# A two-layer attention trunk on one core: the mask of a tenth group on VectorE, other buffer counts, another order of issue

## The chip, the core and the metric

The kernel runs on one core of one Trainium2 chip. A core has TensorE (PE) for matmuls, VectorE (DVE), ScalarE (ACT) and GpSimd (POOL) for elementwise work, and SyncE (SP), which here issues all the transfers between memory and the core's on-chip buffers. Each engine runs its own list of instructions in order and waits for others at semaphores. The metric is the time of one execution on the device, in microseconds (us); lower is better.

## The reference

The input x is 256 tokens by 1024 in float32. Two layers run one after the other, and then a final RMSNorm:

```
h = x
for i in 0, 1:
    hn = rmsnorm(h, norm_g[i])
    q, k, v, z = split(hn @ w_in[i])           # 16 heads of 64
    q, k = rope(q), rope(k)
    o = attention_i(q, k, v)                   # see below
    h = h + (o * silu(z)) @ w_out[i]
out = rmsnorm(h, final_g)
```

Layer 0 has 2 key heads, a sliding window of 128 keys, and one learned logit per head (a sink) that takes part in the softmax. Layer 1 has 4 key heads and attends in blocks of 256 keys; with 256 tokens there is only the token's own block, so it is plain causal attention. All weights are float32.

## The kernel before

**Weights.** The weights stream through the core once, in chunks of 128x1024 (512 KB). `load` (L90) takes a raw buffer `wraw` (one of NRAW) and lets SP issue the transfer. `split` turns a chunk into two of a reduced matmul format: ScalarE copies it to `whi` (L114), and VectorE subtracts that from the raw chunk to give `wlo` (L115); there are NHI and NLO buffers of these. Each copy waits for the subtraction of the chunk before it (PACE). Seven chunks (NATIVE) are not split and go to TensorE as they are (L149).

**Projections.** The activations stand transposed in SBUF, as 8 tiles of 128 features by 256 tokens, each split in the same way into a high and a low part (`quad`, L170 and L171). A 128x128 block of weights then takes three matmuls: high by high (L151), high by low (L152), low by high (L153). The same three stand at L290 to L292 for v of layer 1, at L450 to L452 for the output projection of layer 0, and at L487 to L489 for that of layer 1, which is computed in rows.

**Norms.** The norm's factor is taken out of the projections. The squares of the 8 tiles (`square`) are made by GpSimd (L176) for the tiles in SQP and by ScalarE (L178) otherwise, and added up by GpSimd (L181) in NACC accumulators. `stats` sums them over features by matmuls against a column of ones (L190), takes the power -1/2 on GpSimd and spreads the result over the features (L197).

**Attention.** `attn` handles 12 groups (layer, c, b, u): a half c of the heads, a block b of 128 queries, and for b = 1 a quarter u of the heads. A group has four heads with 256 keys, or (b = 0) eight heads with 128 keys. Its steps are:

- scores (`sc`, L351), matmuls with 64 rows of contraction;
- mask and maximum: for the groups in TTM, one VectorE operation a head, which adds the mask, writes the result and keeps the extreme (L355); otherwise two matmuls that add the mask in place (L361) and one VectorE reduction (L363);
- exponentials on ScalarE (L373 for TTM groups, L375 otherwise), reciprocal of the sums (L378), scaling on ScalarE for groups in PSC (L381), on VectorE otherwise (L383);
- transposes on TensorE (`tr`, L389), copied out by VectorE for groups in PEV (L392), by ScalarE otherwise (L394);
- P V products (`o`, L404), matmuls that write 64 columns of the array;
- the gate: times silu(z) (L410), and the split of the result into high (ScalarE, L416) and low (GpSimd for GLP, VectorE otherwise, L417).

silu(z) is made from a tanh (L432 to L438; the last steps on GpSimd for the parts in SZP), the rotary products by VectorE or, for RPL, GpSimd.

**What sets the order.** No order is written out by hand. A scheduler issues each engine's instructions by a priority, and every stage has one: layer times 100 plus an entry of PRI0 or PRI1 (`sq0` the split of q's weights of half 0, `a1` the attention of half 1, `o0` the output projection of half 0, and so on). ORDERS gives the order of the three groups of a half. So the tables of numbers at L24 to L42 decide what stands behind what on each engine.

Of the kernel before, what the change touches and what calls it, by code (L numbers as in the profile page):

```python
# [20 lines left out]
SYNC = mybir.DependencyInfo(mybir.DependencyClass.Sync, mybir.DependencyReason.DATA)  # L21
PACE = 1
NATIVE = (1, 2, 5, 6, 10, 13, 31)
RPL = [(0, 'k'), (0, 0, 0), (1, 'k'), (1, 0, 0), (1, 1, 0)]  # L24
GLP = [(0, 0, 0, 1), (0, 0, 1, 0), (0, 1, 0, 0), (0, 1, 0, 1), (1, 0, 1, 0), (1, 1, 0, 1)]
SZP = [(0, 0, 0), (0, 0, 1), (0, 0, 2), (0, 1, 2), (0, 1, 3), (1, 0, 0), (1, 0, 1), (1, 0, 2), (1, 0, 3), (1, 1, 1), (1, 1, 2)]
PSC = [(0, 0, 0, 0), (0, 0, 0, 1), (0, 0, 1, 0), (0, 0, 1, 1), (0, 1, 1, 1), (1, 0, 1, 0), (1, 0, 1, 1), (1, 1, 0, 0), (1, 1, 1, 0), (1, 1, 1, 1)]
PEV = [(0, 0, 0, 1), (0, 0, 1, 0), (0, 1, 0, 0), (0, 1, 0, 1), (1, 0, 0, 1), (1, 0, 1, 0), (1, 0, 1, 1), (1, 1, 0, 0), (1, 1, 0, 1), (1, 1, 1, 0), (1, 1, 1, 1)]
NRAW, NHI, NLO = 10, 6, 5
PRI0 = {'xf': -37.2, 'hi': -428.1, 'sr': -212.6, 'tr': -201.4, 'skv': -239.2, 'st': -202.2, 'kv': -40.0, 'sq0': 117.0, 'q0': 61.8, 'sz0': -423.6, 'z0': 22.4, 'a0': -231.3, 'sq1': 114.4, 'q1': -33.8, 'a1': -409.0, 'sz1': -356.7, 'z1': 57.5, 'so0': -315.8, 'o0': 144.9, 'so1': 106.2, 'o1': -413.8, 'r0': -105.6, 'r1': 19.7, 'rk': -221.8, 'p0': 21.4, 'p1': -32.3, 'e0': -419.0, 'e1': -270.7, 'f0': -176.2, 'f1': -172.3}  # L30
PRI1 = {'xf': -32.2, 'r0': 100.5, 'r1': 41.1, 'tr': 65.9, 'skv': 75.5, 'st': 15.9, 'kv': -179.8, 'sq0': -132.0, 'q0': 96.7, 'sz0': -35.0, 'z0': 217.1, 'a0': 44.0, 'sq1': -436.9, 'q1': 120.3, 'a1': -261.3, 'sz1': -243.0, 'z1': 33.9, 'so0': 29.9, 'o0': 69.6, 'so1': -254.9, 'o1': 34.0, 'rk': -306.8, 'p0': 14.1, 'p1': -192.3, 'e0': 71.7, 'e1': -119.0, 'f0': -280.2, 'f1': -10.4}
NPT = 6
NMM, NTR, NSC = 3, 2, 1
NW = 9
ORDERS = [[[(1, 0), (0, 0), (1, 1)], [(1, 0), (0, 0), (1, 1)]], [[(0, 0), (1, 1), (1, 0)], [(0, 0), (1, 1), (1, 0)]]]
STEP = 0.1
TTM = [(0, 0, 1, 0), (0, 0, 1, 1), (0, 1, 0, 0), (0, 1, 1, 0), (0, 1, 1, 1), (1, 0, 0, 0), (1, 0, 1, 1), (1, 1, 0, 0), (1, 1, 1, 1)]
SQP = [(0, 0), (0, 1), (0, 3), (0, 5), (1, 1), (1, 5), (1, 6)]
NACC = [2, 2]
PVZ = 0  # L40
EPS = 1e-05
NEG = -1e+30  # L42
# [3 lines left out]
def trunk(ctx: ExitStack, tc: tile.TileContext, xT, gf, sinks, consts, masks, wkva, w, out):  # L46
# [7 lines left out]
    @contextmanager  # L54
    def at(p):
        old = tc.cur_priority
        tc.cur_priority = int(p * 1000)
        yield
        tc.cur_priority = old
# [98 lines left out]
    def split_h(layer, k, hs):  # L158
        whole = any(26 * layer <= j < 26 * layer + 20 for j in NATIVE)
        if k == 0:  # L160
            xf.append(act.tile([P, KT, S], F32, name="xf", bufs=1) if whole else None)
        if k % 2 == 0:
            q = quads()
            hs += [q[:, 0], q[:, 1]]
        hi, lo = hs[k][:, 0], hs[k][:, 1]
        gc = g[:, layer, k:k + 1]
        if whole:
            with at(100 * layer + (PRI0, PRI1)[layer]["xf"] + 0.5 * k):
                nc.scalar.activation(xf[layer][:, k], h[:, k], AF.Copy, scale=gc)  # L169
        nc.scalar.activation(hi, h[:, k], AF.Copy, scale=gc)  # L170
        nc.vector.scalar_tensor_tensor(lo, h[:, k], gc, hi.bitcast(F32), op0=OP.mult, op1=OP.subtract)  # L171

    def square(layer, k):
        q = work.tile([P, S], F32, name="sq", bufs=4)
        if (layer, k) in SQP:
            nc.gpsimd.tensor_mul(q, h[:, k], h[:, k])  # L176
        else:
            nc.scalar.activation(q, h[:, k], AF.Square)  # L178
        if k >= NACC[layer]:
            a = acc[layer][k % NACC[layer]]  # L180
            nc.gpsimd.tensor_add(a, a, q)  # L181
        else:
            acc.setdefault(layer, []).append(q)
# [18 lines left out]
    for k in range(KT):  # L202
        with at(PRI0["hi"] + 0.5 * k):
            split_h(0, k, hs)
        with at(PRI0["sr"] + 0.5 * k):
            square(0, k)

    for layer in range(2):
# [8 lines left out]
        B = 100 * layer  # L217
        PRI = (PRI0, PRI1)[layer]

# [12 lines left out]
        def rope(aps, pool=False, out=None):  # L232
            n = sum(x.shape[1] for x in aps)
            t1 = work.tile([P, n, S], F32, name="t1") if out is None else out
            t2 = work.tile([P, n, S], F32, name="t2")
            n = 0
            for x in aps:
                m = x.shape[1]
                nc.vector.stream_shuffle(t2[:, n:n + m], x, [(i + 16) % 32 for i in range(32)])
                nc.vector.tensor_mul(t1[:, n:n + m], x, csr[:, 0, None].to_broadcast([P, m, S]))  # L240
                n += m
            eng = nc.gpsimd if pool else nc.vector
            eng.tensor_mul(t2, t2, csr[:, 1, None].to_broadcast([P, n, S]))
            eng.tensor_add(t1, t1, t2)
            return t1
# [54 lines left out]
        def q_part(c, pq):  # L300
            qs = act.tile([P, 4, S], F32, name="qs", bufs=2)
            for u in range(2):
                rope(pq[u], (layer, c, u) in RPL, qs[:, 2 * u:2 * u + 2])
            return qs
# [7 lines left out]
        tc.cur_priority = int(1000 * (B + PRI["rk"]))  # L312
        kr = rope([pk[:, :nkv // 2]], (layer, "k") in RPL)
        for i in range(2):
# [16 lines left out]
        def attn(c, b, u, qs):  # L331
# [14 lines left out]
            sc = psum.tile([P, 2, 512], F32, name="sc", bufs=NSC).rearrange("p r (i k) -> p r i k", i=np_)  # L346
            wide = (layer, c, b, u) in TTM
            for n in range(nh):
# [30 lines left out]
            for n in range(nh):  # L379
                if (layer, c, b, u) in PSC:  # L380
                    nc.scalar.activation(p[:, n], p[:, n], AF.Copy, scale=ri[:, n:n + 1])  # L381
# [3 lines left out]
            for j in range(2):  # L385
# [4 lines left out]
                pT = work.tile([P, 4, P], F32, name="pT", bufs=NPT)  # L390
                if (layer, c, b, u) in PEV:
                    ie = nc.vector.tensor_copy(pT, pt)  # L392
# [18 lines left out]
            for v in us:  # L411
# [4 lines left out]
                last[0] = nc.scalar.activation(gh, gv, AF.Copy)  # L416
                (nc.gpsimd if (layer, c, v, b) in GLP else nc.vector).tensor_sub(gl, gv, gh.bitcast(F32))  # L417

        def zproj(c):
            with at(B + PRI["sz%d" % c]):  # L420
                hw = split(jz[c])
            with at(B + PRI["z%d" % c]):
                for f in range(4):
# [5 lines left out]
                    with at(B + PRI["e%d" % c]):  # L429
# [3 lines left out]
                        nc.scalar.activation(th, z, AF.Tanh)  # L433
                        if (layer, c, f) in SZP:
                            nc.gpsimd.tensor_mul(th, th, z)  # L435
# [76 lines left out]
        def attn_c(c, qs):  # L512
            for i, (b, u) in enumerate(ORDERS[layer][c]):
                with at(B + PRI["a%d" % c] + STEP * i):
                    attn(c, b, u, qs)
# [84 lines left out]
```

## Time and profile before

| | us |
|---|---|
| median of 3 runs (219.52 to 219.86) | 219.74 |
| the profiled execution | 219.47 |
| its span, first to last instruction on the core | 217.7 |
| TensorE busy | 210.3 |
| VectorE busy | 156.0 |
| ScalarE busy | 137.8 |
| GpSimd busy | 59.5 |

The profiled execution is one run under the hardware profiler; its time exceeds the span by what lies before the first and after the last recorded instruction. Busy is the time in which an engine works on an instruction. An engine whose busy time is nearly the span can still be waiting in one place; what it waits for is told by the view of waits, and what a single piece adds to the end by the chain of waits, which goes back from the last instruction to whatever released it.

### The profile page before, as it was taken

Reading aid. Unit: us, or ns where it says so; the run is one execution under the profiler, and the core shown is the slowest. Engines: PE = TensorE matmul, PEld = TensorE weight load, DVE = VectorE, ACT = ScalarE, POOL = GpSimd, SP = SyncE. Lnnn points to the kernel's source line nnn. Section 1 sums busy time; section 2 is a strip of 40 time slices with the busy share of each in tenths; the row PEclk is TensorE's granted clock in tenths of the full one; section 3 lists DMA queues with packets and bytes.
Section 4 is the critical chain, followed back from the end, with each engine's and each line's share of the span. In section 5 each row is a group of like instructions: output and inputs, shape, how many; then the busy total and the mean of one; then the engine's idle time right before and its main releaser. Section 6 shows DMA issues by size and latency. Waiting matters only on the chain.

```text
span 217.7 us, 4176 instructions
## 1 busy us (share of the span) xinstructions
PE 210.3 (97%) x1533; PEld 185.4 (85%) x1533; DVE 156.0 (72%) x359; ACT 137.8 (63%) x335; POOL 59.5 (27%) x67
## 2 busy tenths in 40 slices
PE   8999999999999999999999999999999999999990
PEld 3879999896798989899999999999799997777780
DVE  3437978987488995768864577799655998585462
ACT  6683179698879576429931554567888997352221
POOL 2561440014401046003920182130440047000331
PEclk9999999999999999999999999999999999999998
DMA  6999999365041336345552664643530000000022
GB/s 173 278 386 411 408 400 321 133 199 184 5 148 47 96 98 193 105 131 161 190 144 89 211 232 114 222 120 133 172 118 3 0 3 0 0 0 3 0 96 96
DMA packets 10244, 31.71 MB, mean 146 GB/s; under 512 B 1264, under 2 KB 2160, under 8 KB 10224
## 3 DMA queue, kind: packets, MB, share of 16 engines
q1 hardware_dynamic: 10224, 31.45, 43.3%
q8 instruction: 12, 0.20, 0.3%
q14 instruction: 8, 0.07, 0.1%
HBM read 30.39 MB, written 1.05 MB: 144 GB/s over the span
## 4 chain that ended last, share of the span: by engine, by line
PE 89%; DMA 2%; SPq 2%; DVE 2%; issue 1%; ACT 1%; POOL 1%; POOLq 0%
PE mm L151 13%; PE mm L153 12%; PE mm L152 12%; PE mm L149 9%; PE sc L351 6%; PE o L404 6%; PE tr L389 5%; PE mm L451 4%; PE mm L452 4%; PE mm L450 4%; PE mm L487 3%; PE mm L489 3%; PE mm L488 2%; DMA hg<-xT 2%; SPq L96 1%
## 5 line engine op out<-in xcount | busy, mean ns | idle before, releaser
L115 DVE TENSOR_TENSOR wlo<-wraw,whi 128x1024 fp32r<-128x1024 f32 (+2 forms) x49 | 62.2, 1272 | 17.2 <-ACT whi L114 13.8
L114 ACT ACTIVATE whi<-wraw 128x1024 fp32r<-128x1024 f32 (+2 forms) x49 | 49.6, 1021 | 38.8 <-DVE wlo L115 18.3
L151 PE MATMUL mm<-quad,whi 128*128 128x256 f32 x224 | 66.4, 298 | 0.4 <-ACT whi L114 0.4
L152 PE MATMUL mm<-quad,whi 128*128 128x256 f32 x224 | 64.4, 288 | 0.0
L153 PE MATMUL mm<-quad,wlo 128*128 128x256 f32 x224 | 64.0, 288 | 0.0
L151 PEld LDWEIGHTS mm<-quad,whi 128*128 128x128 f32 x224 | 42.8, 191 | 2.3 <-issue 1.1
L153 PEld LDWEIGHTS mm<-quad,wlo 128*128 128x128 f32 x224 | 42.6, 191 | 1.2 <-issue 1.1
L152 PEld LDWEIGHTS mm<-quad,whi 128*128 128x128 f32 x224 | 42.8, 191 | 0.7
L435 POOL TENSOR_TENSOR th<-th,z 128x256 f32<-128x256 f32 x11 | 10.3, 936 | 56.2 <-ACT th L433 56.2
L373 ACT ACTIVATE p<-p,nm 128x256 f32<-128x256 f32 (+1 forms) x48 | 21.3, 444 | 5.0 <-DVE nm L355 4.9
L149 PE MATMUL mm<-xf,wraw 128*128 128x256 f32 x96 | 23.3, 380 | 0.3 <-ACT xf L169 0.3
L149 PEld LDWEIGHTS mm<-xf,wraw 128*128 128x128 f32 x96 | 17.3, 190 | 2.5 <-ACT xf L169 0.6
L452 PE MATMUL mm<-quad,wlo 128*128 128x256 f32 x64 | 18.4, 287 | 0.0
L451 PE MATMUL mm<-quad,whi 128*128 128x256 f32 x64 | 18.3, 286 | 0.0
L450 PE MATMUL mm<-quad,whi 128*128 128x256 f32 x64 | 18.3, 286 | 0.0
L381 ACT ACTIVATE p<-p,ri 128x256 f32<-128x256 f32 (+1 forms) x44 | 16.8, 458 | 1.4 <-DVE ri L378 1.3
L389 PE MATMUL tr<-cst,p 128*128 128x128 f32 x96 | 15.4, 273 | 0.0
L351 PE MATMUL sc<-ks,qs 64*128 64x256 f32 (+1 forms) x128 | 15.2, 348 | 0.0
L171 DVE SCALAR_TENSOR_TENSOR quad<-hg,quad 128x256 fp32r<-128x256 f32 x16 | 9.3, 601 | 6.5 <-ACT quad L170 6.5
L487 PE MATMUL mm<-whi,quad 128*128 128x512 f32 (+2 forms) x36 | 13.9, 385 | 0.0
L404 PE MATMUL o<-pT,vs 128*64 128x256 f32 x96 | 13.7, 395 | 0.0
L488 PE MATMUL mm<-wlo,quad 128*128 128x512 f32 (+2 forms) x36 | 13.3, 373 | 0.0
(110 smaller groups left out, 378.0 us busy)
## 6 DMA issues: line engine op xcount, KB each, us to landing
wraw<-w SPq DMA_DIRECT2D x50, 512.0 KB, 4.7
wraw<-wkva SPq DMA_DIRECT2D x2, 512.0 KB, 8.4
out<-of SPq DMA_DIRECT2D x4, 256.0 KB, 2.2
wraw<-w SPq DMA_DIRECT2D x3, 256.0 KB, 3.9
hg<-xT SPq DMA_DIRECT2D x2, 256.0 KB, 6.0
wraw<-gf SPq DMA_DIRECT2D x1, 512.0 KB, 3.6
hg<-xT SPq DMA_DIRECT2D x3, 128.0 KB, 3.4
cst<-consts SPq DMA_DIRECT2D x1, 320.0 KB, 8.5
```

Source lines behind the costliest of these rows:

```text
L114: ia = nc.scalar.activation(a[:, c0:c1], r[:, c0:c1], AF.Copy)
L115: ib = nc.vector.tensor_sub(b[:, c0:c1], r[:, c0:c1], a[:, c0:c1].bitcast(F32))
L149: nc.tensor.matmul(ps, wh, x, start=start, stop=stop)
L151: nc.tensor.matmul(ps, wh, xh, start=start, stop=False)
L152: nc.tensor.matmul(ps, wh, xl, start=False, stop=False)
L153: nc.tensor.matmul(ps, wl, xh, start=False, stop=stop)
L351: nc.tensor.matmul(sc[:, par, i], qs[half, 2 * us[0] + i, b * P:(b + 1) * P], ks[half, (h0 + n) // per, :nk], start=i == 0, stop=wide and ...
L389: nc.tensor.transpose(pt[:, n], p[:, n0 + n, kt * P:(kt + 1) * P], ident)
L404: im = nc.tensor.matmul(po[64 * par:64 * par + 64, i0:i0 + 2], vs[:, kt, (h0 + 2 * i0) // per], pTs[j][:, par::2], start=st, stop=sp)
L450: nc.tensor.matmul(ps, wh, gh, start=k == 0, stop=False)
L451: nc.tensor.matmul(ps, wh, gl, start=False, stop=False)
L452: nc.tensor.matmul(ps, wl, gh, start=False, stop=k == 3)
```

## The change

The change touches only tables of numbers, at the same lines as before. The mask of group (1, 1, 1, 0), the last of the kernel, moves from TensorE to VectorE (TTM, nine groups to ten). The raw weight buffers go from 10 to 7, the high ones from 6 to 8. Two squares of layer 0 go from GpSimd to ScalarE (SQP). The squares of layer 1 are added up in one accumulator, not two (NACC). Scaling on ScalarE (PSC) takes in the groups (0,1,0,0) and (0,1,1,0). The evictions in PEV, the gate's low parts in GLP, the rotary products in RPL and the last steps of silu in SZP are dealt out differently between VectorE, ScalarE and GpSimd. In layer 1 the first half takes its groups in another order (ORDERS). Nearly every priority is different.

```diff
-RPL = [(0, 'k'), (0, 0, 0), (1, 'k'), (1, 0, 0), (1, 1, 0)]
-GLP = [(0, 0, 0, 1), (0, 0, 1, 0), (0, 1, 0, 0), (0, 1, 0, 1), (1, 0, 1, 0), (1, 1, 0, 1)]
-SZP = [(0, 0, 0), (0, 0, 1), (0, 0, 2), (0, 1, 2), (0, 1, 3), (1, 0, 0), (1, 0, 1), (1, 0, 2), (1, 0, 3), (1, 1, 1), (1, 1, 2)]
-PSC = [(0, 0, 0, 0), (0, 0, 0, 1), (0, 0, 1, 0), (0, 0, 1, 1), (0, 1, 1, 1), (1, 0, 1, 0), (1, 0, 1, 1), (1, 1, 0, 0), (1, 1, 1, 0), (1, 1, 1, 1)]
-PEV = [(0, 0, 0, 1), (0, 0, 1, 0), (0, 1, 0, 0), (0, 1, 0, 1), (1, 0, 0, 1), (1, 0, 1, 0), (1, 0, 1, 1), (1, 1, 0, 0), (1, 1, 0, 1), (1, 1, 1, 0), (1, 1, 1, 1)]
-NRAW, NHI, NLO = 10, 6, 5
+RPL = [(0, 0, 0), (0, 0, 1), (0, 1, 1), (1, 'k'), (1, 0, 0)]
+GLP = [(0, 0, 1, 1), (0, 1, 0, 0), (0, 1, 1, 1), (1, 0, 0, 0), (1, 0, 1, 1), (1, 1, 1, 0), (1, 1, 1, 1)]
+SZP = [(0, 0, 1), (0, 0, 2), (0, 0, 3), (0, 1, 3), (1, 0, 1), (1, 1, 0), (1, 1, 1), (1, 1, 3)]
+PSC = [(0, 0, 0, 0), (0, 0, 1, 0), (0, 0, 1, 1), (0, 1, 0, 0), (0, 1, 0, 1), (0, 1, 1, 0), (0, 1, 1, 1), (1, 0, 0, 1), (1, 0, 1, 0), (1, 0, 1, 1), (1, 1, 0, 0), (1, 1, 0, 1), (1, 1, 1, 0), (1, 1, 1, 1)]
+PEV = [(0, 0, 0, 1), (0, 0, 1, 0), (0, 1, 0, 1), (0, 1, 1, 0), (0, 1, 1, 1), (1, 0, 0, 1), (1, 0, 1, 1), (1, 1, 0, 0), (1, 1, 0, 1), (1, 1, 1, 1)]
+NRAW, NHI, NLO = 7, 8, 5
...
-ORDERS = [[[(1, 0), (0, 0), (1, 1)], [(1, 0), (0, 0), (1, 1)]], [[(0, 0), (1, 1), (1, 0)], [(0, 0), (1, 1), (1, 0)]]]
+ORDERS = [[[(1, 0), (0, 0), (1, 1)], [(1, 0), (0, 0), (1, 1)]], [[(0, 0), (1, 0), (1, 1)], [(0, 0), (1, 1), (1, 0)]]]
...
-SQP = [(0, 0), (0, 1), (0, 3), (0, 5), (1, 1), (1, 5), (1, 6)]
-NACC = [2, 2]
+SQP = [(0, 0), (0, 3), (1, 1), (1, 5), (1, 6)]
+NACC = [2, 1]
```

(TTM gains the entry (1, 1, 1, 0); PRI0 and PRI1 have 31 and 29 numbers each, and what they move is shown by the order of the instructions.)

The groups with b = 0 all have u = 0, so an entry (layer, c, 0, 1) of PSC or PEV names no group.

On TensorE, at the scores of the third group of layer 0 (`sc_758`), with the P V products of the first group (`o_680`), before the change:

```order
L153 MATMUL mm_595<-quad_219,wlo_546 128x256
L351 MATMUL sc_758<-ks_417,qs_401 128x256
L404 MATMUL o_680<-pT_671,vs_416 64x256 x2
L351 MATMUL sc_758<-ks_417,qs_401 128x256
L404 MATMUL o_680<-pT_678,vs_416 64x256 x2
L351 MATMUL sc_758<-ks_417,qs_401 128x256 x2
L151 MATMUL mm_595<-quad_219,whi_545 128x256
```

and after it:

```order
L153 MATMUL mm_571<-quad_256,wlo_542 128x256
L404 MATMUL o_680<-pT_671,vs_416 64x256 x2
L404 MATMUL o_680<-pT_678,vs_416 64x256 x2
L351 MATMUL sc_758<-ks_417,qs_401 128x256 x4
L151 MATMUL mm_594<-quad_219,whi_545 128x256
```

The two kinds alternated, and now all products stand ahead of all scores.

On TensorE, in the first half of layer 1, the P V products of its first group (`o_1982`, `o_1977` after the change) and the scores of its last (`sc_2044`, `sc_2038`); before:

```order
L404 MATMUL o_1982<-pT_1973,vs_1545 64x256 x2
L153 MATMUL mm_1837<-quad_1347,wlo_1795 128x256
L151 MATMUL mm_1837<-quad_1388,whi_1794 128x256
L152 MATMUL mm_1837<-quad_1388,whi_1794 128x256
L153 MATMUL mm_1837<-quad_1388,wlo_1795 128x256
L351 MATMUL sc_2044<-ks_1546,qs_1654 128x256 x2
L404 MATMUL o_1982<-pT_1980,vs_1545 64x256 x2
L351 MATMUL sc_2044<-ks_1546,qs_1654 128x256 x2
L361 LDWEIGHTS mkb_72
L361 MATMUL sc_2044<-mkb_72 128x2x128
```

and after:

```order
L404 MATMUL o_1977<-pT_1968,vs_1543 64x256 x2
L404 MATMUL o_1977<-pT_1975,vs_1543 64x256 x2
L389 MATMUL tr_2011<-cst_71,p_1993 128x128 x4
L389 MATMUL tr_2018<-cst_71,p_1993 128x128 x4
L351 MATMUL sc_2038<-ks_1544,qs_1652 128x256 x4
L152 MATMUL mm_1895<-quad_1266,whi_1796 128x256
```

Transposes of the second group now stand between the products and the scores, and this last group's mask is on VectorE, the second's on TensorE.

On TensorE, at the end of layer 1, the transposes of the last group's probabilities (`p_2331`) and what stands around them after the change:

```order
L404 MATMUL o_2070<-pT_2061,vs_1543 64x256 x2
L404 MATMUL o_2070<-pT_2068,vs_1543 64x256 x2
L389 MATMUL tr_2305<-cst_71,p_2286 128x128 x4
L389 MATMUL tr_2312<-cst_71,p_2286 128x128 x4
L404 MATMUL o_2270<-pT_2261,vs_1543 64x256 x2
L404 MATMUL o_2270<-pT_2268,vs_1543 64x256 x2
L389 MATMUL tr_2350<-cst_71,p_2331 128x128 x4
L389 MATMUL tr_2357<-cst_71,p_2331 128x128 x4
L487 MATMUL mm_2443<-whi_2401,quad_1987 128x512
```

and before it, where that group's probabilities are `p_2335`:

```order
L488 MATMUL mm_2431<-wlo_2413,quad_1992 128x512
L389 MATMUL tr_2353<-cst_71,p_2335 128x128 x4
L389 MATMUL tr_2360<-cst_71,p_2335 128x128 x4
L404 MATMUL o_2075<-pT_2066,vs_1545 64x256 x2
L404 MATMUL o_2075<-pT_2073,vs_1545 64x256 x2
L489 MATMUL mm_2431<-whi_2412,quad_1992 128x512
L487 MATMUL mm_2431<-whi_2412,quad_1992 128x512
```

The last group's transposes move to behind the products of two earlier groups. Between its scores and its transposes there are now 16 matmuls of the output projection, 16 transposes and these eight products.

## Rows read from the trace of the kernel before

**Rows 1.** The page's head: span, then busy us, share and count by engine.
```profile
span 217.7 us, 4176 instructions
PE 210.3 (97%) x1533; PEld 185.4 (85%) x1533; DVE 156.0 (72%) x359; ACT 137.8 (63%) x335; POOL 59.5 (27%) x67
```
**Rows 2.** Waits of TensorE: what was waited for, us in all, times, longest.
```profile
PE mm L75 <- DVE mhalf L138: 1.0, 1, 1.0
...
PE mm L149 <- ACT xf L169: 0.3, 1, 0.3
```
**Rows 3.** Chain of waits, 48 to 60 us: start, us, what (records joined).
```profile
49.21 0.63 PE sc L351 x2
49.84 0.58 PE o L404 x4
...
51.63 0.63 PE sc L351 x4
52.26 0.31 PE mm L151
...
57.33 0.12 PE mm L152
57.44 1.06 PE sc L351 x8
58.51 1.01 PE o L404 x8
```
**Rows 4.** Chain of waits, 88 to 90 us.
```profile
88.01 0.58 PE o L404 x4
88.59 0.32 PE mm L451
```
**Rows 5.** Chain of waits, 152 to 156 us.
```profile
152.22 0.58 PE o L404 x4
...
155.32 0.33 PE sc L361 x2
```
**Rows 6.** Chain of waits, at the statistics of layer 1.
```profile
118.81 0.56 PE tr L190 x6
```
**Rows 7.** Groups by line and shape: count, busy us, mean ns of one, idle before.
```profile
L363 DVE TENSOR_REDUCE nm<-sc 128x4 f32<-128x1024 f32 x2 | 2.4, 1207 | 1.1 <-PE sc L361 1.1
L355 DVE CUSTOM_DVE_ANT_0 p<-sc,mkb 128x256 f32<-128x256 f32 x8 | 2.9, 420 | 0.0
L381 ACT ACTIVATE p<-p,ri 128x256 f32<-128x256 f32 x28 | 11.9, 498 | 1.4 <-DVE ri L378 1.3
L381 ACT ACTIVATE p<-p,ri 128x128 f32<-128x128 f32 x16 | 4.9, 388 | 0.0
```
**Rows 8.** Timeline of ScalarE in the front: start, us, what, idle before and releaser.
```profile
12.79 0.91 ACT L170 ACTIVATE quad<-hg 128x256 fp32r<-128x256 f32 x2 [0.63 <-DMA hg<-xT]
```
**Rows 9.** Stretches: us, busy PE, PEld, DVE, ACT, POOL, clock, DMA share, GB/s.
```profile
60.00:87.00 27.00, 27.00 (x223) 24.15 (x222) 22.10 (x71) 20.22 (x59) 6.86 (x7) 1.00 0.38 117
...
165.00:190.00 25.00, 25.00 (x185) 21.50 (x184) 20.17 (x39) 19.45 (x54) 6.82 (x7) 1.00 0.00 1
```
**Rows 10.** Chain of waits, at the last groups of layer 1.
```profile
171.73 1.06 PE sc L351 x8
...
182.29 0.23 PE mm L487
...
186.38 0.87 PE tr L389 x8
```
**Rows 11.** Timeline of ScalarE, at the last group of layer 1.
```profile
177.98 1.05 ACT L114 ACTIVATE whi<-wraw 128x1024 fp32r<-128x1024 f32 x1
...
180.16 1.70 ACT L381 ACTIVATE p<-p,ri 128x256 f32<-128x256 f32 x4
```
**Rows 12.** Waits of SP's queue: us in all, times, longest.
```profile
SPq L90 <- DVE wlo L115: 88.6, 26, 10.0
```
**Rows 13.** DMA issues: count, KB each, median us to landing.
```profile
wraw<-w SPq DMA_DIRECT2D x50, 512.0 KB, 4.7
```

More of the change, by code (lines that the diff above doesn't have):

```diff
@@ L29 @@
-NRAW, NHI, NLO = 10, 6, 5
-PRI0 = {'xf': -37.2, 'hi': -428.1, 'sr': -212.6, 'tr': -201.4, 'skv': -239.2, 'st': -202.2, 'kv': -40.0, 'sq0': 117.0, 'q0': 61.8, 'sz0': -423.6, 'z0': 22.4, 'a0': -231.3, 'sq1': 114.4, 'q1': -33.8, 'a1': -409.0, 'sz1': -356.7, 'z1': 57.5, 'so0': -315.8, 'o0': 144.9, 'so1': 106.2, 'o1': -413.8, 'r0': -105.6, 'r1': 19.7, 'rk': -221.8, 'p0': 21.4, 'p1': -32.3, 'e0': -419.0, 'e1': -270.7, 'f0': -176.2, 'f1': -172.3}
-PRI1 = {'xf': -32.2, 'r0': 100.5, 'r1': 41.1, 'tr': 65.9, 'skv': 75.5, 'st': 15.9, 'kv': -179.8, 'sq0': -132.0, 'q0': 96.7, 'sz0': -35.0, 'z0': 217.1, 'a0': 44.0, 'sq1': -436.9, 'q1': 120.3, 'a1': -261.3, 'sz1': -243.0, 'z1': 33.9, 'so0': 29.9, 'o0': 69.6, 'so1': -254.9, 'o1': 34.0, 'rk': -306.8, 'p0': 14.1, 'p1': -192.3, 'e0': 71.7, 'e1': -119.0, 'f0': -280.2, 'f1': -10.4}
+RPL = [(0, 0, 0), (0, 0, 1), (0, 1, 1), (1, 'k'), (1, 0, 0)]
@@ new lines @@
+NRAW, NHI, NLO = 7, 8, 5
+PRI0 = {'xf': -140.3, 'hi': -409.9, 'sr': -212.6, 'tr': -377.4, 'skv': -239.2, 'st': -276.2, 'kv': -128.3, 'sq0': -105.7, 'q0': 120.5, 'sz0': -188.9, 'z0': 42.6, 'a0': -276.5, 'sq1': 155.1, 'q1': -123.7, 'a1': -333.1, 'sz1': 118.6, 'z1': 48.0, 'so0': -208.8, 'o0': 213.0, 'so1': -418.6, 'o1': -142.3, 'r0': -221.9, 'r1': -402.2, 'rk': -401.0, 'p0': -334.1, 'p1': -375.3, 'e0': 96.9, 'e1': 65.3, 'f0': -371.0, 'f1': -225.3}
+PRI1 = {'xf': -48.2, 'r0': -288.2, 'r1': 71.6, 'tr': 41.1, 'skv': 52.6, 'st': 51.0, 'kv': 38.2, 'sq0': -203.3, 'q0': 67.5, 'sz0': 300.2, 'z0': 199.7, 'a0': 51.7, 'sq1': 100.8, 'q1': 78.3, 'a1': -193.7, 'sz1': 30.5, 'z1': 31.5, 'so0': 90.5, 'o0': -18.9, 'so1': 301.8, 'o1': 115.5, 'rk': 40.9, 'p0': 73.3, 'p1': 64.4, 'e0': -163.9, 'e1': 303.1, 'f0': -328.7, 'f1': -54.0}
@@ L34 @@
 NW = 9
-ORDERS = [[[(1, 0), (0, 0), (1, 1)], [(1, 0), (0, 0), (1, 1)]], [[(0, 0), (1, 1), (1, 0)], [(0, 0), (1, 1), (1, 0)]]]
+ORDERS = [[[(1, 0), (0, 0), (1, 1)], [(1, 0), (0, 0), (1, 1)]], [[(0, 0), (1, 0), (1, 1)], [(0, 0), (1, 1), (1, 0)]]]
 STEP = 0.1
-TTM = [(0, 0, 1, 0), (0, 0, 1, 1), (0, 1, 0, 0), (0, 1, 1, 0), (0, 1, 1, 1), (1, 0, 0, 0), (1, 0, 1, 1), (1, 1, 0, 0), (1, 1, 1, 1)]
-SQP = [(0, 0), (0, 1), (0, 3), (0, 5), (1, 1), (1, 5), (1, 6)]
-NACC = [2, 2]
+TTM = [(0, 0, 1, 0), (0, 0, 1, 1), (0, 1, 0, 0), (0, 1, 1, 0), (0, 1, 1, 1), (1, 0, 0, 0), (1, 0, 1, 1), (1, 1, 0, 0), (1, 1, 1, 0), (1, 1, 1, 1)]
+SQP = [(0, 0), (0, 3), (1, 1), (1, 5), (1, 6)]
+NACC = [2, 1]
 PVZ = 0
```

## The prediction

> **What bounds the kernel now.** I read the page's head first: a span of 217.7 us, in which TensorE is busy for 210.3 us, VectorE for 156.0 and ScalarE for 137.8 [rows 1]. A share of 97% does not yet say that TensorE sets the time, since an engine can be slow to start and wait at the end, so I went to its waits next. There are three, from 1.0 us down to 0.3 [rows 2], and all three lie in the first 13 us (the first load and the first splits). After that every stretch that I cut out shows TensorE busy for its whole length at a granted clock of 1.00, for instance 27.00 of 27.00 us and 25.00 of 25.00 [rows 9], while VectorE and ScalarE each have 4.8 to 6.8 us free there. So from 13 us to the last matmul the time is simply the sum of what TensorE issues. A microsecond taken off another engine is worth nothing; a microsecond off TensorE is worth a whole one, until another engine is no longer in time.
>
> The chain of waits then shows what a piece of TensorE's row costs. It writes each matmul's share of the end. A 128x256 matmul that follows its like costs 0.12 us. The first one after a block of 64-row scores (L351) or 64-column P V products (L404) costs 0.31 to 0.32 instead [rows 3, 4]. Four scores in a row (eight records) cost 1.06, and the four P V products right behind them 1.01; but a single score between two P V products costs 0.63, just as much as two scores together, and two P V products cost 0.58 [rows 3]. So the same instructions cost more the more often they alternate. That is what the change has to be read for.
>
> **The change, part by part.** The program does the same arithmetic; what differs is which engine does some elementwise work, and the order in which everything is issued. On TensorE:
>
> 1. Third group of layer 0, first half. Before, the order is score, two P V, score, two P V, two scores: 0.63 + 0.58 + 0.63 + 0.58 + 0.63 = 3.05 us (two of the five rows stand in the group twice over, 49.21 to 52.26) [rows 3]. In the changed order the four P V products stand together and the four scores right behind them, as the pair at 57.44 does the other way round: 1.06 + 1.01 = 2.07. The matmul behind pays 0.31 in both. Gain 0.98.
>
> 2. Last P V block of layer 0. Before: two, a matmul of the output projection, two more, another matmul: 0.58 + 0.32 twice, 1.80 us [rows 4]. After: four together, then two matmuls: 1.01 + 0.32 + 0.12 = 1.45. Gain 0.35.
>
> 3. Layer 1, first half. Before, from 152.22 to 155.65: two P V, four projection matmuls (0.31 and three of 0.12), two scores, two P V, two scores, two mask matmuls, in all 3.43 us [rows 5]. After: the four P V, eight transposes, the four scores, then projection matmuls. For the same instructions that is 1.01 + 1.06 + 0.31 + three of 0.12 = 2.74, and 0.2 to 0.33 for the second way in and out, so 2.94 to 3.07; I take a gain of 0.40. The mask matmuls move to another group of this half and cost there 0.33 less the 0.19 that the matmul behind them no longer pays, 0.14 more; the two that the tenth VectorE group saves at the end of the layer give 0.33 less the 0.2 of entering what now follows, 0.13. These cancel.
>
> 4. The statistics of layer 1 sum one accumulator instead of two: four records fewer, of the kind of which six cost 0.56 us in a row [rows 6], so 0.37.
>
> Together 0.98 + 0.35 + 0.40 + 0.37 = 2.10 us.
>
> On the other engines, what hides each edit:
>
> 5. Mask of the last group on VectorE: one reduction of 1.21 us goes, four mask operations of 0.42 come [rows 7], 0.5 more on VectorE, which has 4.8 us free of 25 in that stretch [rows 9]. Cost nothing while the transposes of this group come late enough (rival C).
>
> 6. Squares 1 and 5 of layer 0 go from GpSimd to ScalarE, at no more than the 0.50 that a 128x256 operation takes there [rows 7]. ScalarE stood idle for 0.63 us for pieces of the input [rows 8], so I take nothing; uncovered, the two would cost 1.0.
>
> 7. Scalings of two groups of layer 0 go to ScalarE: eight of 128x128 at 0.39 and four of 128x256 at 0.50 [rows 7], at most 5.1 us more (two evictions go the other way). ScalarE has 20.22 of 27 us filled there [rows 9]; 25.3 of 27 still fits, so I take nothing, with one quartet of scalings, 1.70 us [rows 11], as the other bound (rival B).
>
> 8. Gate lows, rope products and silu products change between VectorE and GpSimd. GpSimd is busy for under 7 of 27 us [rows 9], so it has room both ways. Nothing, and below nothing is no end either, since TensorE waits for none of them.
>
> 9. Raw weight buffers 10 to 7, high ones 6 to 8. SP issues a chunk when its buffer is free, for which it waits 88.6 us in all [rows 12], and the data land 4.7 us later [rows 13]. TensorE needs about 4 us per chunk (some 200 us for 50 chunks), so seven buffers can still be some 28 us ahead of it, less the time that a chunk waits in its raw buffer to be split. I take nothing, with 1 us as the other bound, for the stretch around 30 us where the loads have only just got ahead.
>
> The profiled execution took 219.47 us, of which 217.7 are the span, and 219.47 - 2.10 = 217.37. The median of the three runs shown is 219.74, 0.27 above the profiled one, so on that footing 217.64.
>
> A rule of the Trainium skill bears on points 1 to 3. By its page "TensorEngine Tiling (Array Packing)", section Tiling Modes (Key Properties), "Mode switching requires drain": to go from the full array to half-array tiles empties the engine. The rows agree that a first matmul behind such a block takes 0.31 rather than 0.12. By that rule alone, with each change of mode priced at this 0.19, point 1 saves three changes, 0.57 us rather than 0.98; the rest of the 0.98 is that a lone score takes as long as two, which the rule does not say. The sum would then be 1.7, and the time 218.0.
>
> **The rivals.**
>
> A, the forecast: nothing new waits, TensorE's row is 2.10 us shorter. For it speaks that TensorE waits nowhere now after 13 us, and that the others have idle time in every stretch. Against it: everything on ScalarE and VectorE is reordered, and I cannot see in the order what slack is left.
>
> B: the scalings that move to ScalarE hold back a split or a P V group in layer 0. For it: ScalarE goes to over 90% of 60 to 87 us. The price is up to a quartet of scalings, 1.70; I take three quarters of it, 1.3. 217.64 + 1.3 = 218.9, still a little faster.
>
> C, the one that ends slower: the last groups pile up at the end. Before, the last group's transposes come at 186.38, 13.6 us behind the end of its scores at 172.79 [rows 10]. In the new order there stand between these two 16 output matmuls of 0.23 (182.29), 16 transposes (two blocks of 0.87, as at 186.38) and two P V blocks of 1.01: 3.7 + 1.7 + 2.0 and some 0.4 for the ways in, 7.85 us. The softmax of that group ended at 180.16 + 1.70 = 181.86 before, 9.07 us behind its scores. ScalarE did 2.2 us of other work between that group's exponentials and its scalings, from 177.98 to 180.16 [rows 11], which the new order has elsewhere, and VectorE needs 0.5 more for the masks: about 7.4, in time by 0.5. If that other work is in the way again or the masks wait behind a split on VectorE, TensorE waits for the difference, up to 13.6 - 7.85 = 5.75 us if the group takes as long as it was given before. From 2.5 us of wait on (2.1 and the 0.44 of the margin) the change is slower: 220.2 to 223.4.
>
> D: with seven raw buffers a chunk comes late. For it: SP waits for a free buffer 26 times as it is [rows 12]. Against: the lead of point 9. 1 to 3 us, so 218.6 to 220.6.
>
> E: the alternation is no loss but cover; scores between P V products let VectorE start sooner, and what the order saves comes back as waits. No gain: 219.7.
>
> **How the numbers follow.** What a measurement of this kernel can tell from no change is about 0.2%, 0.44 us, so 219.3 to 220.2 is "same". Chances: A 0.55, B 0.15, C 0.15, D 0.07, E 0.08. A's own range is 217.0 to 218.5: 0.4 to either side for the sizes of points 1 to 4 (block 3 above all, and 218.0 for the smaller price of a change), the rest for the 0 to 1.0 of point 6. The range goes from 216.9 to 220.3, and leaves out C's upper part and a little below. Faster: A 0.55, B 0.12, D 0.03, E 0.01, together 0.71. Slower: C 0.12, B 0.01, D 0.02, E 0.01, together 0.16. Same: the other 0.13.
>
> **What would show it.** In the changed profile the chain should have a P V block of 1.01 and a score block of 1.06 back to back near 49 us, one P V block of 1.01 near 87 us, and a statistics block of about 0.4 near 118 us; the first matmul of the last output projection half should stand some 2 us sooner, and the tail behind the last matmul should be as long as before. Wrong would be: a wait of TensorE over 0.5 us behind 13 us. Named L389 behind L381 at the end, it is C; behind L381 or L394 at 60 to 87 us, B; whi or wlo there whose own wait ends with a transfer, D. If the blocks read as I say and TensorE's span is no shorter with no wait shown, the price of alternation is wrong.

## The result, and the profile after

The changed kernel takes 217.19 us (median of 6 runs, 216.49 to 217.45) where the kernel before takes 219.47 in the same session (6 runs, 218.87 to 219.86): a ratio of 0.9895, with a 95% interval of 0.9874 to 0.9915. It is faster by 1.0%. The forecast was 217.6. The profiled executions stand at 217.45 and 219.47. One execution of a version below, the profiled one of E3, took 715.83 us at a granted clock of 1.00, with all of TensorE's instructions stretched (the matmuls of L152 took 680 ns on the mean, 288 in the kernel before); why is not known, and it is left out of E3's figures.

The page's head of the changed kernel, against [rows 1], and its waits of TensorE, against [rows 2]:

```profile
span 215.7 us, 4169 instructions
PE 208.6 (97%) x1527; PEld 185.1 (86%) x1527; DVE 152.3 (71%) x354; ACT 141.9 (66%) x351; POOL 58.4 (27%) x61
```

```profile
PE mm L75 <- DVE mhalf L138: 1.0, 1, 1.0
PE mm L149 <- ACT xf L169: 0.2, 1, 0.2
```

ScalarE is 4 us busier, VectorE 4 us less, and neither matters: TensorE still waits nowhere behind the first 13 us, so from there on the time is what TensorE issues. The chain of waits of the changed kernel, at the places of [rows 3, 4] and at the statistics of layer 1 [rows 6] (start, us, what):

```profile
49.37 1.01 PE o L404 x8
50.39 1.06 PE sc L351 x8
51.45 0.32 PE mm L151
...
87.75 1.01 PE o L404 x8
88.77 0.32 PE mm L450
...
117.75 0.34 PE tr L190 x4
```

The block that took 3.05 us takes 2.08 (49.37 to 51.45), the last P V block 1.01 and one way out, the statistics 0.34 for four records.

A measure that the start of the kernel does not move is the stretch from the first statistics matmul of layer 0 (L190) to the start of the last matmul. Its ends in the timeline of TensorE, in the kernel before and in the changed one:

```profile
15.77 1.03 PE L190 MATMUL tr<-one,sq 128*128 128x2 f32 x8
...
211.69 0.28 PE L489 MATMUL mm<-whi,quad 128*128 128x128 f32 x1
```

```profile
16.28 0.99 PE L190 MATMUL tr<-one,sq 128*128 128x2 f32 x8
...
209.66 0.28 PE L489 MATMUL mm<-whi,quad 128*128 128x128 f32 x1
```

That is 195.92 us before and 193.38 after: TensorE's row lost 2.54 us. The changed kernel's front, up to the statistics, was 0.51 longer in this execution, and the difference of the spans is 2.0. From here on "the row" is this stretch, told for every experiment. It differed by 0.06 us among the three kernels below that have one and the same order on TensorE (the changed one, E5 and E6); its first piece, the eight records of the statistics, took 0.95 to 1.07 us from one profile to the next.

### The profile page after: what moved, and what is told of

Same layout as the page of the kernel before. It is cut to its first block, busy times and chain, and to the rows that moved or that the text cites. A ratio compares the mean times of both kernels' runs of the same rounds, so it can differ in the third digit from the quotient of the medians.

```text
span 215.7 us, 4169 instructions
## 1 busy us (share of the span) xinstructions
PE 208.6 (97%) x1527; PEld 185.1 (86%) x1527; DVE 152.3 (71%) x354; ACT 141.9 (66%) x351; POOL 58.4 (27%) x61
## 4 chain that ended last, share of the span: by engine, by line
PE 89%; DMA 3%; SPq 2%; issue 2%; DVE 1%; POOL 1%; ACT 1%; POOLq 0%
PE mm L153 13%; PE mm L151 13%; PE mm L152 12%; PE mm L149 9%; PE sc L351 6%; PE o L404 6%; PE tr L389 5%; PE mm L450 4%; PE mm L452 4%; PE mm L451 4%; DMA hg<-xT 3%; PE mm L489 3%; PE mm L487 3%; PE mm L488 3%; SPq L96 1%
## 5 line engine op out<-in xcount | busy, mean ns | idle before, releaser
L115 DVE TENSOR_TENSOR wlo<-wraw,whi 128x1024 fp32r<-128x1024 f32 (+2 forms) x49 | 59.5, 1217 | 18.2 <-ACT whi L114 15.0
L152 PE MATMUL mm<-quad,whi 128*128 128x256 f32 x224 | 64.6, 289 | 0.0
L152 PEld LDWEIGHTS mm<-quad,whi 128*128 128x128 f32 x224 | 43.1, 192 | 1.1 <-issue 0.7
L435 POOL TENSOR_TENSOR th<-th,z 128x256 f32<-128x256 f32 x8 | 7.7, 962 | 61.8 <-ACT th L433 57.8
L149 PE MATMUL mm<-xf,wraw 128*128 128x256 f32 x96 | 23.2, 381 | 0.3 <-ACT xf L169 0.2
L373 ACT ACTIVATE p<-p,nm 128x256 f32<-128x256 f32 (+1 forms) x52 | 23.1, 448 | 0.1
L381 ACT ACTIVATE p<-p,ri 128x256 f32<-128x256 f32 (+1 forms) x56 | 21.0, 452 | 1.0 <-DVE ri L378 1.0
L149 PEld LDWEIGHTS mm<-xf,wraw 128*128 128x128 f32 x96 | 17.3, 190 | 3.0 <-ACT xf L169 1.1
L389 PE MATMUL tr<-cst,p 128*128 128x128 f32 x96 | 16.1, 275 | 0.0
L243 POOL TENSOR_TENSOR t<-t,csr 128x512 f32<-128x512 f32 x5 | 8.3, 1669 | 21.6 <-DVE t L239 14.4
L351 PE MATMUL sc<-ks,qs 64*128 64x256 f32 (+1 forms) x128 | 14.0, 345 | 0.0
L487 PE MATMUL mm<-whi,quad 128*128 128x512 f32 (+2 forms) x36 | 13.7, 380 | 0.0
L489 PE MATMUL mm<-whi,quad 128*128 128x512 f32 (+2 forms) x36 | 13.6, 378 | 0.0
```

Source lines behind the costliest of these rows:

```text
L115: ib = nc.vector.tensor_sub(b[:, c0:c1], r[:, c0:c1], a[:, c0:c1].bitcast(F32))
L149: nc.tensor.matmul(ps, wh, x, start=start, stop=stop)
L152: nc.tensor.matmul(ps, wh, xl, start=False, stop=False)
L351: nc.tensor.matmul(sc[:, par, i], qs[half, 2 * us[0] + i, b * P:(b + 1) * P], ks[half, (h0 + n) // per, :nk], start=i == 0, stop=wide and ...
L373: nc.scalar.activation(p[:, n], p[:, n], AF.Exp, bias=nm[:, n:n + 1], scale=-1.0, accum_out=rs[:, n:n + 1])
L389: nc.tensor.transpose(pt[:, n], p[:, n0 + n, kt * P:(kt + 1) * P], ident)
```

## The experiments

The theory T: TensorE's row sets the time; a block of scores or of P V products costs more the more pieces it comes in; and all that the other engines were dealt is hidden. Against it stood that the priorities bring the gain by when things are ready (P), that the moved work and the buffers bring it (R), and the prediction's C, D and E.

Each table has the row in us, worked out from the two timeline rows of that kernel's profile, and the ratio to the kernel before in the same session.

**E1 and E2, priorities alone and tables alone.** E1 is the kernel before with `PRI0`, `PRI1` and `ORDERS` of the changed kernel; E2 the changed kernel with those three of before. The edit of E1, cut to the short line:

```diff
...
-ORDERS = [[[(1, 0), (0, 0), (1, 1)], [(1, 0), (0, 0), (1, 1)]], [[(0, 0), (1, 1), (1, 0)], [(0, 0), (1, 1), (1, 0)]]]
+ORDERS = [[[(1, 0), (0, 0), (1, 1)], [(1, 0), (0, 0), (1, 1)]], [[(0, 0), (1, 0), (1, 1)], [(0, 0), (1, 1), (1, 0)]]]
...
```

> The kernel before with the changed kernel's priorities and group orders alone; its buffers, masks, accumulators and shares of the engines are those of before. Its row on TensorE splits more blocks than before: one group of scores and P V products of layer 0 alternates five ways, another P V block comes in pieces of one and two. Theory T (TensorE's row sets the time, and each block of scores or products costs more the more pieces it comes in): the pieces sum to 1.4 us more than before by the prices 1.06 and 1.01 for four together, 0.58 to 0.63 for a piece and 0.19 for the way out, so about 220.9. Rival P (the priorities as such bring the gain, by when things are ready): about 217.2, as fast as the changed kernel. Rival R (the gain comes from the work that changed engines and from the buffers): 219.5.

> The changed kernel with the priorities and group orders of before; all else as changed. Its row on TensorE has the products and scores of the first disputed block together, the last product block of layer 0 together, one accumulator of statistics, and a few blocks apart that the changed kernel has side by side. Theory T: its pieces sum to 1.6 us less than before, the statistics to 0.4 less, so about 217.5. Rival P: 219.5. Rival R: 217.2. E1 and this one together part T from both.

| | row | us, median | ratio, 95% interval |
|---|---|---|---|
| E1 | 200.97 | 224.48 | 1.0237, 1.0212 to 1.0262 |
| E2 | 195.06 | 218.44 | 0.9953, 0.9938 to 0.9968 |

P falls: the changed kernel's priorities on the tables of before are 2.4% slower, not 1% faster. R falls as the whole story: the tables alone give 0.5%. T has the signs right and misses E1's size. Its chain shows the pieces that were priced, for instance one group of scores and products that alternates five ways:

```profile
71.94 0.63 PE sc L351 x4
72.57 0.58 PE o L404 x4
73.15 0.63 PE sc L351 x2
73.78 0.58 PE o L404 x4
74.36 0.63 PE sc L351 x2
```

but its waits of TensorE show what the price left out:

```profile
PE mm L487 <- ACT quad L416: 1.3, 1, 1.3
...
PE tr L466 <- DVE pT L392: 0.7, 1, 0.7
...
PE mm L151 <- DVE z L432: 0.6, 1, 0.6
```

2.6 us of waits behind the front that neither the kernel before nor the changed one has. The row is 5.05 longer than before; the priced pieces (1.4) and these waits make 4.0 of it, and the other 1.0 was not taken apart. The longest wait is for the gate's high part of a late group, 1.3 us, in the last output projection. The end of the kernel can pile up, then, as the prediction's C has it, but by another wait than C's: C named the transposes (L389) behind the scalings (L381), and these did not wait here. In E2 my expectation had an error of its own: by a second count the pieces listed there add up to 0.6 us less than before, not 1.6, so T should have said 218.4. Measured is 1.03 us less than before by the ratio, and a row 0.86 shorter. That repaired sum was made after the run, so E2 is weaker evidence than the two experiments that follow.

**E3 and E12, two blocks joined in the kernel before.** One edit in the kernel before; the tables stay. E12 is E3's kernel once more, for its profile. The ends of the lines that were added to:

```diff
+PVZ = 0; AFTER = {(0, 0, 1, 1): (0, 1, 0), (1, 0, 1, 0): (0, 0, 0)}
...
+ n == nh - 1 and (layer, c, b, u) in AFTER and tc.add_manual_dep(pvs[AFTER[layer, c, b, u]].ins, isc.ins.name, LATE, reason="behind")
...
+ pvs.setdefault((c, b, u), im)
```

(`isc` is the score matmul of head n, `im` a P V matmul; the dependence orders them and is of the kind without a semaphore, NoSync.)

> The kernel before with one edit: in two places (the third group of layer 0, the second of layer 1) the P V products are ordered behind the scores of the group that they alternated with, so that four scores and four products stand together. One other block comes apart by it. Theory T: 0.98 less at the first place, 0.53 more at the block that comes apart, 0.54 less at the second place, about 1.0 less: 218.5. By a price of 0.19 for every way in and out alone (a lone score no dearer than one of four): about 0.5 less, 219.0. Rival E of the prediction (the alternation hides waits): 219.5.

> E3 again for its profile. Theory T: four scores and four products of the third group of layer 0 in a row at 1.06 and 1.01, the same at the second group of layer 1, no new wait of TensorE, and from the statistics of layer 0 to the last matmul 194.9 where before had 195.9.

E3 is 218.32 us, ratio 0.9956 (0.9938 to 0.9974), by the ratio 0.96 us less than before; T had 1.0, the price of the ways in and out alone 0.5, E nothing. E12's chain:

```profile
48.99 1.06 PE sc L351 x8
50.05 1.01 PE o L404 x8
...
55.17 1.06 PE sc L351 x8
56.23 0.32 PE mm L153
...
57.14 0.58 PE o L404 x4
...
58.04 0.58 PE o L404 x4
...
152.33 1.06 PE sc L351 x8
153.40 1.01 PE o L404 x8
```

The two joined blocks stand as priced, and so does the one that came apart at 55.17. The row is 194.85 (15.55 to 210.40); T had 194.9.

**E4, two blocks split in the changed kernel.** The mirror image: in two groups of the changed kernel the second score is ordered behind the first two P V products, the third behind the last two.

```diff
+PVZ = 0; ALT = {(0, 1, 1, 0): (0, 0, 0), (0, 1, 1, 1): (0, 1, 1)}; AT = {1: 0, 2: 1}
...
+ n in AT and (layer, c, b, u) in ALT and tc.add_manual_dep(isc.ins, pvs[ALT[layer, c, b, u] + (AT[n],)].ins.name, LATE, reason="between")
...
+ pvs[c, b, u, j] = im
```

> The changed kernel with one edit: in the two groups of layer 0's second half whose four scores and four products stand together, they alternate as in the disputed block of the kernel before (one score, two products, one score, two products, two scores, one or three projection matmuls behind the first score). Theory T: 1.16 us more at each, so 219.5, all of the gain gone though nothing else is changed. By 0.19 for every way in and out alone: 0.76 at each, 218.7. Rival E: 217.2 as without the edit.

219.13 us, ratio 0.9989 (0.9975 to 1.0004): the gain is gone, though tables and priorities are those of the changed kernel. Its chain at the first of the two:

```profile
56.43 0.63 PE sc L351 x2
57.06 0.31 PE mm L153
57.37 0.58 PE o L404 x4
57.95 0.63 PE sc L351 x2
58.58 0.58 PE o L404 x4
59.16 0.63 PE sc L351 x4
```

The row is 195.69 (16.09 to 211.78), 2.31 more than the changed kernel's; T had 2.3, the price of 0.19 a way 1.5. Rival E falls with E3 and E4. They also part the two prices of the prediction: by 0.19 for each change alone both runs would have moved by only half to two thirds of what they did. A lone score at 0.63 us, as dear as two, makes up the rest. Why it is as dear no run shows. By the page "TensorEngine Tiling (Array Packing)" of the Trainium skill, section Tiling Modes (Key Properties), a change of mode drains TensorE. The cost at each way out of a block (0.31 for 0.12) agrees with that; the price of a lone score it does not give.

**E5, E6, E8: buffers, squares, one accumulator.** Three edits of the changed kernel, each with the row's order unchanged (in E8 but for the matmuls that go):

```diff
-NRAW, NHI, NLO = 7, 8, 5
+NRAW, NHI, NLO = 10, 6, 5
```

```diff
-SQP = [(0, 0), (0, 3), (1, 1), (1, 5), (1, 6)]
+SQP = [(0, 0), (0, 1), (0, 3), (0, 5), (1, 1), (1, 5), (1, 6)]
```

```diff
-NACC = [2, 1]
+NACC = [1, 1]
```

> The changed kernel with 10 raw and 6 high buffers as before; TensorE's order is the same instruction by instruction. Theory T: no wait of TensorE hangs on the buffers, so the same time as the changed kernel, 0.989 of before, 217.0. Rival D of the prediction (with seven raw buffers a chunk is late somewhere): faster than the changed kernel by what it waited, 216.0 to 216.7. On the front: the changed kernel's statistics of layer 0 began at 16.28 us, 0.5 later than before (15.77). If the buffer counts did that, they begin near 15.8 here and the time is 0.5 less; if not, near 16.2.

> The changed kernel with the two squares of layer 0 back on GpSimd; TensorE's order is the same. If the two added ScalarE operations delay the front (point 6 of the prediction took nothing, 1.0 at most), the statistics of layer 0 begin near 15.8 us, not 16.28, and the time is 0.5 less: 216.5. If the input's landing sets the front, which differs from run to run, the same as the changed kernel, 217.0.

> The changed kernel with one accumulator of squares in layer 0 too, as it has in layer 1; two matmuls of the statistics (four records) go, the order is otherwise the same. Theory T: 0.4 us less, 216.6, if GpSimd's sums are in time. Rival W: the sums of the front are already the last thing that these matmuls wait for, and GpSimd has one more addition of 0.73 us to make one behind the other; then TensorE waits for it, and what is saved is lost: 217.0 to 217.4.

| | row | us, median | ratio, 95% interval |
|---|---|---|---|
| changed | 193.38 | 217.19 | 0.9895, 0.9874 to 0.9915 |
| E5 | 193.38 | 217.06 | 0.9893, 0.9875 to 0.9912 |
| E6 | 193.32 | 216.72 | 0.9880, 0.9860 to 0.9901 |
| E8 | 193.07 | 217.18 | 0.9899, 0.9878 to 0.9919 |

E5: the row is the same to the hundredth. Seven buffers are enough, and D falls. E6's time can't be told from the changed kernel's. The statistics began at 15.86 us in E5 and at 15.57 in E6. Either number, by what I had written down for it, would blame the edit for the 0.5 us of the front. But the input landed earlier in both. ScalarE's timeline in the changed kernel, E5, E6 and E8, at the fifth and sixth tile of the input:

```profile
11.05 0.91 ACT L170 ACTIVATE quad<-hg 128x256 fp32r<-128x256 f32 x2 [0.63 <-DMA hg<-xT]
...
12.18 0.89 ACT L169 ACTIVATE xf<-hg 128x256 f32<-128x256 f32 x2
```

```profile
10.64 0.91 ACT L170 ACTIVATE quad<-hg 128x256 fp32r<-128x256 f32 x2 [1.46 <-DMA hg<-xT]
```

```profile
10.35 0.91 ACT L170 ACTIVATE quad<-hg 128x256 fp32r<-128x256 f32 x2 [0.82 <-DMA hg<-xT]
```

```profile
11.35 0.91 ACT L170 ACTIVATE quad<-hg 128x256 fp32r<-128x256 f32 x2 [2.26 <-DMA hg<-xT]
12.16 0.71 ACT L178 ACTIVATE sq<-hg 128x256 f32<-128x256 f32 x2
12.77 0.89 ACT L169 ACTIVATE xf<-hg 128x256 f32<-128x256 f32 x2
```

From there to the statistics it is 16.28 - 11.05 = 5.23 us in the changed kernel, 15.86 - 10.64 = 5.22 in E5 and 15.57 - 10.35 = 5.22 in E6. So neither the buffers nor the two squares cost anything there, and the 0.51 by which the changed kernel's front was longer goes with this landing (11.05, where the kernel before had 10.15).

In E8 it is 5.53: the row is 0.31 shorter as T has it (0.38), the front 0.31 longer, and the time the same. That is the time of W, the rival there, but not its reason. W has TensorE wait for GpSimd's last sum; that sum was done at 14.91 + 1.53 = 16.44, and the statistics began at 16.88, right behind the native matmuls (L149):

```profile
14.91 1.53 POOL L181 TENSOR_TENSOR sq<-sq 128x256 f32<-128x256 f32 x2 [0.68 <-ACT sq L178]
```

Those started later. With one accumulator ScalarE takes two squares in a row (12.16) ahead of the copies that these matmuls read, where the changed kernel has one, and the copies begin 1.42 us behind the tile's start (12.77 - 11.35) and not 1.13 (12.18 - 11.05). That is 0.29 of the 0.31 (TensorE's wait for these copies is 1.6 us in E8, 0.2 in the changed kernel). Whether the saving stays with the squares in the old order was not tried.

**E7 and E11, the mask.** E7 takes (1, 1, 1, 0) out of the changed kernel's TTM, E11 puts it into that of before; nothing else is edited.

```diff
-TTM = [(0, 0, 1, 0), (0, 0, 1, 1), (0, 1, 0, 0), (0, 1, 1, 0), (0, 1, 1, 1), (1, 0, 0, 0), (1, 0, 1, 1), (1, 1, 0, 0), (1, 1, 1, 0), (1, 1, 1, 1)]
+TTM = [(0, 0, 1, 0), (0, 0, 1, 1), (0, 1, 0, 0), (0, 1, 1, 0), (0, 1, 1, 1), (1, 0, 0, 0), (1, 0, 1, 1), (1, 1, 0, 0), (1, 1, 1, 1)]
```

> The changed kernel with the mask of the last group back on TensorE (nine groups in the list, as before); the rest of the tables as changed. The order differs only behind this group's scores. Theory T: the two mask matmuls cost 0.33, and what follows them 0.2 less: 0.1 to 0.2 slower than the changed kernel, 217.2. Rival C of the prediction (masks and softmax of the last groups are what the end waits for): then one reduction instead of four mask operations is 0.5 sooner on VectorE and the time gets less, 216.5 to 216.8.

> The kernel before with the mask of the last group on VectorE, the one edit; TensorE's order is the same but for the two mask matmuls. Theory T: they cost 0.33 and the transposes behind them now pay 0.2 for the way out: from the statistics of layer 0 to the last matmul 195.8 where before had 195.9, no measurable difference in time. Rival C of the prediction: four mask operations, 0.5 us longer than one reduction, come late for the last transposes and TensorE waits: 0.3 or more slower.

E7: row 193.83, 217.50 us, ratio 0.9908 (0.9889 to 0.9927). E11: row 195.66, 219.35 us, ratio 1.0000 (0.9980 to 1.0020). Neither can be told from its neighbour by time. The rows agree in sign: the mask on VectorE takes 0.26 us off the row of before, 0.08 of it in the statistics of layer 0, which have nothing to do with it (0.95 us for 1.03); putting it back adds 0.45 in the changed kernel, where T had 0.1 to 0.2. Of that, 0.05 lies in the same statistics, and 0.27 in one matmul (L487, 0.50 instead of 0.23, at 194.86), whose weight load waited 0.3 us for VectorE's addition (L491); 0.13 is left for the mask. In E11 the eight transposes behind the scores cost 1.02 us:

```profile
171.57 1.06 PE sc L351 x8
172.64 1.02 PE tr L389 x8
```

against 0.87 for eight behind full-array matmuls [rows 10]. So a way out into transposes costs 0.15, not the 0.2 that I had charged, and in E11 the mask gives 0.33 - 0.15 = 0.18. C did not come in either.

**E9 and E10, a version meant to be faster.** E6 with the last unsplit chunk split too, and layer 1's priorities drawn so that the priced row is short; the two differ in those priorities alone.

```diff
-NATIVE = (1, 2, 5, 6, 10, 13, 31)
+NATIVE = (1, 2, 5, 6, 10, 13)
...
```

> The changed kernel with the two squares of layer 0 on GpSimd as in E6, the last unsplit weight chunk (31, of layer 1) split like its neighbours, and priorities of layer 1 chosen so that the priced row of TensorE is short. Eight double matmuls of 0.43 us become eight triples of 0.36, 0.57 less; its blocks of scores and products cost some 0.15 more than the changed kernel's by the prices of T; ScalarE makes eight copies fewer. Theory T: from the statistics of layer 0 to the last matmul 0.4 us less than E6's 193.3, so 192.9, and the time 0.4 less than E6: 216.3. Rival W (what the new order makes late, as in E1, is not in the price): some wait of 0.5 us or more in layer 1, and 216.8 or more.

> As E9 with another set of priorities of layer 1 that comes to the same price with another order at the end. Theory T: 216.3 like E9. Rival W: the two differ from one another by their waits, by 0.5 us or more.

E9: row 196.42, 219.86 us, ratio 1.0019 (1.0004 to 1.0035). E10: row 196.20, 219.60 us, ratio 1.0006 (0.9991 to 1.0021). Both miss T's 216.3 by over 3 us: all of the gain is lost. The rows miss 192.9 by 3.5 and 3.3. E9's longest wait of TensorE, and what VectorE and GpSimd did there:

```profile
PE mm L153 <- DVE wlo L115: 1.8, 2, 1.4
```

```profile
118.11 2.20 DVE L115 TENSOR_TENSOR wlo<-wraw,whi 128x1024 fp32r<-128x1024 f32 x1
...
126.06 1.88 DVE L115 TENSOR_TENSOR wlo<-wraw,whi 128x1024 fp32r<-128x1024 f32 x1
...
129.07 1.23 DVE L115 TENSOR_TENSOR wlo<-wraw,whi 128x1024 fp32r<-128x1024 f32 x1 [1.12 <-ACT whi L114]
```

```profile
117.94 1.29 POOL L243 TENSOR_TENSOR t<-t,csr 128x512 f32<-128x512 f32 x1 [3.89 <-DVE csr L296]
...
125.58 1.28 POOL L243 TENSOR_TENSOR t<-t,csr 128x512 f32<-128x512 f32 x1 [3.23 <-DVE t L239]
```

W of E9 holds: the two subtractions that TensorE waited for (at 120.31 and 127.94) each took 0.7 to 1.0 us longer than the 1.23 of the one behind them, beside a rotary product on GpSimd. That alone makes no wait: in the changed kernel one took 1.90 beside such a product (at 124.20), and TensorE did not wait for it. In E9 it came too late for what TensorE does next. The wait rows explain 1.8 of E9's 3.5; the rest was not taken apart. E10 has the same wait, 2.1 us, and the two rows differ by 0.22, less than the 0.5 that its rival wanted, so neither of E10's readings came true. What the two versions share, the split of chunk 31, can be as much behind the wait as the priorities; they were not tried apart. Of all versions run, the changed kernel and its edits E5 to E8 are the fastest, and their intervals overlap.

## Why the prediction was right

- **The bound.** TensorE waited nowhere behind 13 us and a shorter row came through: joining two blocks takes 1.07 us off the row (E12) and 0.96 off the time (E3), splitting two adds 2.31 to the row and, by the ratios, 2.06 to the time (E4). The stretch from the last matmul's start to the end was 6.0 us in both kernels.
- **Point 1, 0.98:** 3.05 to 2.08 is 0.97, and E12 has the same block at the same price in the kernel before.
- **Point 2, 0.35:** one block of 1.01 and one way out stand there, as priced.
- **Point 4, 0.37:** the statistics of layer 1 were two blocks before (two records at 111.75, six at 118.81) and are one of four now. By the chains their records cost 0.34 less, and one way out of 0.11 is saved too, which I had not counted: 0.45.
- **Point 3, 0.40, and the masks:** here, and in point 4, the sum was too small. The row lost 2.54, not 2.10. The block of point 3 in the changed kernel:

```profile
161.02 1.01 PE o L404 x8
162.03 1.02 PE tr L389 x8
163.06 1.06 PE sc L351 x8
```

The way into the transposes costs 0.15 and the way from them into the scores nothing, where I had charged 0.2 to 0.33 in all; by the chain it is 1.01 + 0.15 + 1.06 + 0.32 and three more matmuls of 0.34 in all, 2.88 against 3.43, so the gain is 0.55. The masks' new place cost the 0.14 that I gave it. At the end of the layer I had 0.13 for the mask alone, and that stands: its group's scores now lead into a projection matmul of 0.43 us instead of 0.23. But of the last five P V blocks all led into such a matmul before, and four lead into transposes now, for 0.15 each and not 0.20. That is 0.20 less, of which 0.05 goes back where another group's scores changed the other way. These terms, 0.15 in the first half and 0.15 at the end, and the 0.08 of point 4 are 0.38 of the 0.44. The rest, 0.06, is no more than the statistics of layer 0 differ from one profile to the next.
- **Points 5 and 8:** nothing, as forecast: TensorE waits nowhere behind the front.
- **Point 6, the squares:** nothing, by the 5.23 us of the changed kernel and the 5.22 of E6.
- **Point 7 and rival B:** ScalarE came to 22.08 of 27 us busy in the stretch of [rows 9], 1.86 more than before and under the 25.3 allowed for, with TensorE full. No version of the kernel tests B by itself; that TensorE has no wait there is what speaks against it:

```profile
60.00:87.00 27.00, 27.00 (x226) 24.20 (x225) 19.54 (x60) 22.08 (x66) 4.84 (x6) 1.00 0.38 118
```

- **Point 9 and rival D:** fell with E5.
- **Rival C:** in the changed kernel the last group's scores end at 181.28, its scalings at 185.97 + 1.71 = 187.68, and its transposes start at 189.09:

```profile
180.22 1.06 PE sc L351 x8
...
189.09 1.02 PE tr L389 x8
```

```profile
185.97 1.71 ACT L381 ACTIVATE p<-p,ri 128x256 f32<-128x256 f32 x4 [0.24 <-DVE ri L378]
```

The room is 7.81 us where 7.85 was forecast, the softmax takes 6.4 where 7.4 was. In time by 1.4, then, more than the 0.5 that I gave it. No run shows C's own wait; E1 shows another one at the same end, for the gate's high part.
- **The front** was no term of the sum. In the profiled pair it took back 0.51 of the 2.54 and made the spans differ by 2.0; that the median moved by 2.28 fits a front that varies from execution to execution. Of the 0.45 between the forecast of 217.64 and the 217.19 measured, 0.27 is its footing: the three runs that it starts from had a median of 219.74, all six of the session 219.47.

So the right step was to price TensorE's row by its blocks. That the gain of 2.10 came out as close to the measured 2.28 as it did is in part luck: a row forecast 0.44 too long met a front that was late in the profiled execution.

## What to carry to other kernels

Where one engine is busy from end to end, price its row instruction by instruction, with the cost of every change between kinds of matmul, and read a reordering as a change of that row; join what alternates, a lone small matmul above all. The price holds only while nothing new is waited for: it was right within 0.1 us of the row in E4, E5, E6, E8 and E12, off by 0.3 to 0.4 in E7 and in the changed kernel itself, and short by over 3 us in E1, E9 and E10, where a new order made something late. So a new order needs its waits read, each time. And measure from a fixed point behind the input's landing, if changes of a few tenths are to be seen: the row repeated to 0.1 us where the time spread over 1 us.

## What the runs showed of the hardware

- VectorE and GpSimd took turns in these operations, of two inputs each. In E9 the product on GpSimd ran from 117.94 to 119.23, and the subtraction that was begun at 118.11 ended at 120.31, 1.08 after it; the second pair likewise, 126.86 and 127.94. Alone it takes 1.23. This agrees with the Trainium skill, "SBUF — State Buffer", section Who interferes with whom: "*only the shared port pair causes contention, and it's an exclusive lock.*" So such a product on GpSimd is not free for VectorE where the two meet.
- A single 64-row score matmul between others takes 0.63 us, two take 0.63 and four 1.06 [rows 3]; E4 and E12 repeat each of these. The P V products go the same way: one alone (two records) takes 0.57 and two take 0.58 (E1, at 66.09 and 68.41); three (six records) take 1.01 (E2, at 67.20), as much as four.
- The input's landing, from transfers issued at the same times to within 0.02 us, put the start of the fifth tile on ScalarE at 9.63 (E2) to 11.35 us (E8).
